# Regrouping the expert units of a mixture-of-experts stage: one 64-slot and two 32-slot experts per unit, large units and memory steps redistributed, half of the scatter moved

## The chip, the cores and the metric

The kernel runs on one core of a Trainium2 chip. The metric is the device time of the whole program in microseconds (us). Before the change it is 1763.9 us (median of three runs, 1759.8 to 1764.26).

The engines are named as in the profile: PE does matrix products (PEld is its weight load), DVE and ACT are the vector and the scalar engine, POOL is the general one, SP issues the loads of weights.

## What is computed

The program is one hybrid layer (sparse attention, a recurrent branch and a mixture of experts on 256 tokens of width 1024), then a second block of two layers with cross attention to a memory of 256 rows. The change touches the mixture of experts only. Cut to that:

```python
scores = sigmoid(hf @ router_w); choice = scores + router_bias
# 4 of 8 groups of experts, then the best 8 of 64 experts per token
top_e = top_k(where(emask, choice, -inf), 8)
gw = scores[top_e] / sum * 2.5
# every token, for each of its 8 experts e:
y[tok] += gw * (silu(h @ exp_gate[e]) * (h @ exp_up[e])) @ exp_down[e]
out = y + swiglu(h, sh_gate, sh_up, sh_down)
# later, for both layers of the second block:
k, v = split(rms_norm(mem) @ xa_wkv)
```

There are 64 experts; `exp_gate[e]` and `exp_up[e]` are 1024 x 256 and `exp_down[e]` is 256 x 1024, in float32: 1 MB each, 3 MB per expert. All 64 are always read, which is 192 loads of 1 MB.

## The kernel before, in words

**Units and pairs.** The expert stage is a list of *units* of 128 token slots. A unit holds one expert with 128 slots (letter H), two experts with 64 slots (S, the first four experts by number, and M) or four experts with 32 slots (L). All experts but the first four are ranked by how many tokens chose them, on the device: the 4 largest are H, the next 32 are M, the last 24 are L. An expert with more tokens than slots is finished in a loop behind the stage (`loop`), which runs no turn when there is no overflow. `GROUPS = "SMMMMLHLMHLMMM"` gives the order; each letter is a *pair* of units, so there are 14 pairs and 28 units, numbered from 0.

**What a unit does on PE.** At the start of a pair `gather` (L1821) makes the transposed tokens of 256 slots by 32 products with a one-hot matrix P, which DVE makes in `onehot` (L1807, L1808). Then per unit: `spread` (L1841) turns the slot weights; `up` (L1875) multiplies the tokens by the gate and then the up weights, 16 products per expert, each expert in its own columns of the array; ACT applies silu and DVE multiplies (f, L1881); `put` (L1914) adds the result of the unit *before* to the four accumulators of the output, 8 products of 512 columns; `turn` (L1889) transposes f and ACT copies it out (fT, L1891); `down` (L1904) multiplies by the down weights, 4 products per expert. So `put` of the unit before stands on PE between `up` and `turn`, in the time in which ACT and DVE make f; nothing stands between `turn` and `down`.

**Loads.** One queue (SP) issues all loads in program order. The loads of unit p+1 are put in front of the work of unit p. Each load takes the next of a ring of 14 buffers of 1 MB (3 base, 6 of `NRING2`, 3 of `NWS`, 2 of `NRING3`), so load n waits until the products that read load n-14 are done. An H unit takes 3 buffers, S and M take 6, L takes 12. For the last three units the base buffers leave the ring (`drop_ring`).

**Memory steps.** The keys and values of the second block's memory (`MemKV`) are worked out inside the stage, in nine steps behind the units of `KV_AT = 7, 9, 10, 11, 13, 14, 16, 17, 19`: a norm (1 load), two key steps and two value steps (2 loads each), then the same of the second layer but for its last value step, which runs behind the stage. Behind unit 8 stands `further()`, which plans the overflow on DVE and PE.

Of the kernel before, what the change touches and what calls it, by code (L numbers as in the profile page):

```python
# [10 lines left out]
F32 = mybir.dt.float32  # L11
# [4 lines left out]
OP = mybir.AluOpType  # L16
# [285 lines left out]
def flat(t):  # L302
    return t.rearrange("p k t -> p (k t)")
# [196 lines left out]
def mlp(K, layer, nm, nxt):  # L500
# [31 lines left out]


# [982 lines left out]
def first_h2(K, rs, rows, hh, hl):  # L1516


    nc, a = K.nc, K.a
    s2, b2 = rows  # L1520
    both = K.branch.tile([128, 2, D], F32, name="w", tag="w", bufs=2)
    for h in range(2):
        h2 = both[:, h]
        nc.vector.scalar_tensor_tensor(h2, K.X[:, h], rs[:, h:h + 1], s2, op0=OP.mult, op1=OP.mult)
        nc.vector.tensor_add(h2, h2, b2)
        v = h2.rearrange("p (q j) -> p j q", j=8)
        nc.scalar.activation(hh[:, h], v, AF.Copy)
# [26 lines left out]
NRING0, NRING2, NRING3, NRING4 = 6, 6, 2, 2  # L1554


NS, NH, NM, NL, NX = 4, 4, 32, 24, 32
C_PERM, C_FURTHER, NCOL = 64, 128, 128 + NX + 2
GROUPS = "SMMMMLHLMHLMMM"
KV_AT = 7, 9, 10, 11, 13, 14, 16, 17, 19  # L1560
FURTHER = 4


class Moe:
# [14 lines left out]
    def start(self):  # L1579

        K, nc, a = self.K, self.nc, self.a
        nc.gpsimd.dma_start(self.io, a["c_iota"])
        nm = K.nm2
        rs = nm.rows()
        PE, ACT = K.PE, K.ACT
        K.open("route", "right", cur=True)
        first_h2(K, rs, K.h2rows, self.hh, self.hl)
        next(K.parts[0], None)
        lT = K.t([64, T], "lgT")
        nc.scalar.activation(lT, K.lbank[:64, :T], AF.Copy)  # L1590
        lg = K.bank()
        for h in range(2):
            nc.tensor.transpose(lg[:, h * 64:h * 64 + 64], lT[:, h * 128:h * 128 + 128], K.ident[:64, :64])
        with K.after(PE):
            next(K.parts[1], None)
        up = [K.bank("acc") for _ in range(2)]
        rest = shared_in(K, "sh_up", up)
        next(rest)
        row = nm.row()
        s = K.t([128, 2, T], "shs")  # L1600
        self.hidden(K.gate, s, row, True)
        with K.after(PE):
            self.route(lg, rs)
        plan = self.plan()
        next(plan)
        self.take("S", tags=("tmp", "tmp", "acc"))
        next(plan, None)
        next(rest, None)
        self.hidden(up, s, row, False)
        with K.spare():  # L1610
            self.s = [K.t([128, 2, T], "sh" + p, 1, FR) for p in "hl"]
            K.split_into(*(flat(t) for t in self.s), flat(s))
        self.w = K.wload(a["sh_down"][0], 0, 2, 0, D)
        self.first = self.weights([0, 1])
# [182 lines left out]
                else:  # L1797
                    nc.vector.tensor_copy(o, b[:, h * NX:h * NX + NX])

    def onehot(self, col, n, w):  # L1800

        K, nc = self.K, self.nc
        sh = [128, 2, n, w]
        P, Pw = (K.t([128, 2, 256], x, 2, dt, pool=K.moep) for x, dt in (("P", FR), ("Pw", F32)))
        p, pw = (x[:, :, :n * w].rearrange("p h (n w) -> p h n w", w=w) for x in (P, Pw))
        pos, gw = (x[:, :, col:col + n][:, :, :, None].to_broadcast(sh) for x in (self.POS, self.GW))
        nc.vector.tensor_tensor(p, self.io[:, None, None, :w].to_broadcast(sh), pos, op=OP.is_equal)  # L1807
        nc.vector.tensor_tensor(pw, p.bitcast(F32), gw, op=OP.mult)  # L1808
        return P, Pw

    def gather(self, P, w, tags=("tmp",)):
# [16 lines left out]
                nc.scalar.activation(o, bv, AF.Copy)  # L1828
        return X

    def take(self, g, c=0, n=4, tags=("tmp",)):

        P, Pw = self.onehot(c + (C_PERM if g != "S" else 0), n, 256 // n)
        self.taken = self.gather(P, 256, tags), Pw

    def spread(self, Pw, unit):
# [25 lines left out]
                    d[n] = t.rearrange("p (j n) -> p j n", j=8)  # L1862
        return res

    def up(self, X, Pw, i, W):


        K, nc = self.K, self.nc
        C, g = self.spread(Pw, i)
        b = K.bank()  # L1870
        w = 128 // len(W)
        for x, n in enumerate(("exp_gate", "exp_up")):
            for k in range(8):
                for e, d in enumerate(W):
                    nc.tensor.matmul(b[w * e:w * e + w, x * 256:x * 256 + 256],  # L1875
                                     X[:, k, i * 128 + w * e:i * 128 + w * e + w], d[n][:, k],
                                     start=(x == 0 and k == 0), stop=(k == 7), skip_group_check=True)
        s = K.t([128, 256], "fs")
        nc.scalar.activation(s, b[:, 0:256], AF.Silu)  # L1879
        f = K.t([128, 256], "ff", 2)  # L1880
        nc.vector.scalar_tensor_tensor(f, b[:, 256:512], g, s, op0=OP.mult, op1=OP.mult)  # L1881
        return f, C
# [8 lines left out]
        nc.scalar.activation(flat(fT), b[:, :256], AF.Copy)  # L1891
        return fT

    def down(self, fT, W):

        K, nc = self.K, self.nc
        oh, ol = (K.t([128, 2, 512], "o" + p, 2, FR) for p in "hl")
        w = 128 // len(W)
        for n in range(2):
            b = K.bank()  # L1900
            for k in range(2):
                for e, d in enumerate(W):
                    s = slice(w * e, w * e + w)
                    nc.tensor.matmul(b[s], fT[:, k, s], d["exp_down"][:, k, n * 512:n * 512 + 512], start=(k == 0),  # L1904
                                     stop=(k == 1), skip_group_check=True)
            K.split_into(oh[:, n], ol[:, n], b)
        return oh, ol

    def put(self, C, parts, last=False):

        for h in range(2):
            for n in range(2):
                for x, o in enumerate(parts):
                    self.nc.tensor.matmul(self.y[2 * n + h], C[:, h * 128:h * 128 + 128], o[:, n], start=False,  # L1914
                                          stop=(last and x == 1), skip_group_check=True)

    def run(self, steps):

        K = self.K
        first = {"S": 0, "H": NS, "M": NS + NH, "L": NS + NH + NM}  # L1920
        units = []
        for g in GROUPS:
            n = {"H": 2, "L": 8}.get(g, 4)
            for i in range(2):
                units.append((g, first[g], n, [first[g] + i * n // 2 + e for e in range(n // 2)]))
            first[g] += n
        assert first == {"S": NS, "H": NS + NH, "M": NS + NH + NM, "L": 64}
        W, done = [self.first], None

        def load(p):  # L1930
            g, _, _, at = units[p]
            W.append(self.weights([r if g == "S" else self.idp[0:1, r:r + 1] for r in at]))

        for p, (g, c, n, _) in enumerate(units):
            if p % 2 == 0:
                if p:
                    self.take(g, c, n)
                X, Pw = self.taken
            more = steps[KV_AT.index(p)] if p in KV_AT else None
            if more:  # L1940
                more[0].load(more[1])
            if p + 1 < len(units):
                load(p + 1)
            w = W.pop(0)
            f, C = self.up(X, Pw, p % 2, w)
            with K.after(K.PE):
                if done:
                    self.put(*done)
                done = C, self.down(self.turn(f), w)
                if more:  # L1950
                    with K.after(K.PE):
                        more[0].step(more[1])
            if p == 2 * FURTHER:
                self.further()
            if p + 1 == len(units) - 3:
                self.end = self.ahead()
                K.drop_ring(K.ring)
        self.put(*done)
# [16 lines left out]
    def loop(self, end):  # L1975

        K, nc = self.K, self.nc
        with K.tc.For_i(0, end, 1):
            P, Pw = self.onehot(C_FURTHER, 2, 64)
            X = self.gather(P, 128)  # L1980
            W = self.weights([self.idx[0:1, e:e + 1] for e in range(2)])
            f, C = self.up(X, Pw, 0, W)
            self.put(C, self.down(self.turn(f), W))
# [139 lines left out]
```

## Time and profile before

| | |
|---|---|
| median of 3 runs | 1763.9 us |
| the profiled execution | 1768.93 us, span 1767.2 us |
| PE busy | 1678.5 us, 95% of the span |
| DVE, ACT, POOL busy | 834.3, 653.0, 85.7 us |
| moved by DMA | 418.99 MB, mean 237 GB/s |
| expert stage, first `up` to the end of the last `down` | 426.7 to 1004.8 us of the span |
| mean granted PE clock | 0.98 |

Busy time on PE is a sum of overlapping records, so 95% does not say that nothing could be saved there. The timeline gives, for one engine, start and duration of each instruction or run of like instructions, with the idle time before it and what ended that in brackets. A float32 product is recorded as two instructions: a `down` of M (8 products) is x16. The windows give busy time, granted clock and the share of the DMA engines for stretches of the span; a share of 1.00 or a little over means that the 16 DMA engines were never without a packet.

### The profile page before, as it was taken

How to read it: one execution, taken by the hardware profiler on the slowest of the kernel's cores; microseconds unless marked ns; L12 is line 12 of the kernel's file. 1: busy time of each engine (PE TensorE's matmuls, PEld its weight loads, DVE VectorE, ACT ScalarE, POOL GpSimd, SP SyncE). 2: the span in 40 equal slices, each digit the busy share in tenths (PEclk: the TensorE clock that was granted, in tenths of full speed). 3: DMA queues.
4: the chain of work that ended last, by engine and by line, in shares of the span. 5: the costliest groups of instructions: out<-in, count | busy, mean ns of one | idle time of the engine just before them, and what ended most of it. 6: DMA issues, size and time to landing. Idle time of an engine off the chain costs nothing. (4 is left out here: it accounts for less than half of the span.)

```text
span 1767.2 us, 27737 instructions
## 1 busy us (share of the span) xinstructions
PE 1678.5 (95%) x11326; PEld 1275.9 (72%) x11326; DVE 834.3 (47%) x1514; ACT 653.0 (37%) x1105; POOL 85.7 (5%) x105
## 2 busy tenths in 40 slices
PE   5999999998999999899989999999999999999997
PEld 2967667785566666467545577788999877989996
DVE  2664596675222211111112355666555667665554
ACT  2432444552112101211111255756444445554443
POOL 2000000103000000000000020202000000000000
PEclk9989799998999999999999999999999999999999
DMA  9454552583999799899699863546555533445551
GB/s 357 157 167 154 182 164 95 213 300 134 416 416 411 293 369 412 332 409 415 223 416 416 333 204 118 169 138 207 183 189 191 169 119 116 148 143 189 180 181 59
DMA packets 138317, 418.99 MB, mean 237 GB/s; under 512 B 10666, under 2 KB 17588, under 8 KB 118732
## 3 DMA queue, kind: packets, MB, share of 16 engines
q1 hardware_dynamic: 126272, 396.39, 61.0%
q0 software_dynamic: 4336, 12.34, 2.1%
q10 hardware_dynamic: 7580, 8.47, 1.7%
q8 instruction: 90, 1.47, 0.3%
q14 instruction: 39, 0.32, 0.1%
HBM read 410.88 MB, written 6.32 MB: 236 GB/s over the span
## 5 line engine op out<-in xcount | busy, mean ns | idle before, releaser
L153 DVE TENSOR_TENSOR w<-w 128x1024 fp32r<-128x1024 f32 (+1 forms) x283 | 347.2, 1229 | 263.3 <-ACT w L152 262.4
L152 ACT ACTIVATE w<-w 128x1024 fp32r<-128x1024 f32 (+1 forms) x285 | 300.0, 1054 | 317.0 <-PE acc L188 225.0
L1875 PE MATMUL tmp<-w 128*64 128x256 f32 (+2 forms) x2048 | 212.3, 391 | 8.7 <-DMA w<-in_exp_up_dram 7.9
L1875 PEld LDWEIGHTS tmp<-w 128*64 128x64 f32 (+2 forms) x2048 | 132.9, 133 | 79.2 <-issue 10.7
L188 PE MATMUL acc<-hTh,w 128*128 128x256 f32 (+2 forms) x552 | 160.5, 291 | 1.2 <-DVE w L153 1.2
L187 PE MATMUL acc<-hTl,w 128*128 128x256 f32 (+2 forms) x552 | 160.8, 292 | 0.2 <-DVE hTl L153 0.2
L186 PE MATMUL acc<-hTh,w 128*128 128x256 f32 (+2 forms) x552 | 159.9, 290 | 0.8 <-ACT hTh L152 0.7
L186 PE MATMUL tmp<-hTh,w 128*128 128x256 f32 x512 | 145.0, 283 | 0.0
L187 PE MATMUL tmp<-hTl,w 128*128 128x256 f32 x512 | 145.0, 283 | 0.0
L188 PE MATMUL tmp<-hTh,w 128*128 128x256 f32 x512 | 144.8, 283 | 0.0
L1904 PE MATMUL tmp<-w,fT 128*64 128x512 f32 (+2 forms) x512 | 111.3, 598 | 13.3 <-ACT fT L1891 13.3
L187 PEld LDWEIGHTS acc<-hTl,w 128*128 128x128 f32 (+1 forms) x552 | 106.8, 194 | 6.7 <-issue 5.8
L186 PEld LDWEIGHTS acc<-hTh,w 128*128 128x128 f32 (+1 forms) x552 | 106.8, 194 | 5.8 <-issue 4.2
L188 PEld LDWEIGHTS acc<-hTh,w 128*128 128x128 f32 (+1 forms) x552 | 106.7, 194 | 4.8 <-issue 2.6
L1881 DVE SCALAR_TENSOR_TENSOR ff<-tmp,gsl,fs 128x256 f32<-128x256 f32 x28 | 13.5, 483 | 188.6 <-ACT fs L1879 188.6
L187 PE MATMUL acc<-w,gh 128*128 128x512 f32 x256 | 102.2, 399 | 0.0
L186 PE MATMUL acc<-w,gh 128*128 128x512 f32 x256 | 100.9, 394 | 0.0
L188 PE MATMUL acc<-w,gl 128*128 128x512 f32 x256 | 100.5, 392 | 0.0
L153 DVE TENSOR_TENSOR ol<-tmp,oh 128x512 fp32r<-128x512 f32 x56 | 38.6, 690 | 128.2 <-ACT oh L152 128.1
L186 PEld LDWEIGHTS tmp<-hTh,w 128*128 128x128 f32 x512 | 97.9, 191 | 0.6
L187 PEld LDWEIGHTS tmp<-hTl,w 128*128 128x128 f32 x512 | 97.9, 191 | 0.5
L188 PEld LDWEIGHTS tmp<-hTh,w 128*128 128x128 f32 x512 | 98.0, 191 | 0.0
(633 smaller groups left out, 2917.6 us busy)
## 6 DMA issues: line engine op xcount, KB each, us to landing
w<-in_exp_gate_dram SPq DMA_DIRECT2D x64, 1024.0 KB, 13.3
w<-in_exp_up_dram SPq DMA_DIRECT2D x64, 1024.0 KB, 15.3
w<-in_exp_down_dram SPq DMA_DIRECT2D x64, 1024.0 KB, 13.4
w<-in_mlp_w_dram SPq DMA_DIRECT2D x64, 1024.0 KB, 5.3
w<-in_w_in_dram SPq DMA_DIRECT2D x23, 1024.0 KB, 6.0
adaw<-in_ada_w_dram SPq DMA_DIRECT2D x16, 1024.0 KB, 4.9
w<-in_xa_wkv_dram SPq DMA_DIRECT2D x16, 1024.0 KB, 11.0
w<-in_sb_w_in_dram SPq DMA_DIRECT2D x12, 1024.0 KB, 5.1
```

Source lines behind the costliest of these rows:

```text
L152: self.nc.scalar.activation(hi, src, AF.Copy)
L153: self.sub.tensor_tensor(lo, src, hi.bitcast(F32), op=OP.subtract)
L186: mm(out, lh, rh, start=first, stop=False, skip_group_check=True)
L187: mm(out, lh, rl, start=False, stop=False, skip_group_check=True)
L188: mm(out, ll, rh, start=False, stop=last, skip_group_check=True)
L1875: nc.tensor.matmul(b[w * e:w * e + w, x * 256:x * 256 + 256], X[:, k, i * 128 + w * e:i * 128 + w * e + w], d[n][:, k], start=(x == 0 and ...
L1881: nc.vector.scalar_tensor_tensor(f, b[:, 256:512], g, s, op0=OP.mult, op1=OP.mult)
L1904: nc.tensor.matmul(b[s], fT[:, k, s], d["exp_down"][:, k, n * 512:n * 512 + 512], start=(k == 0), stop=(k == 1), skip_group_check=True)
```

## The change

The experts are cut otherwise: 24 M and 32 L instead of 32 M and 24 L. A new unit X holds one M and two L experts (64 + 32 + 32 slots), so it takes 9 buffers. The order is `"SXXHXXMXXHXXM"`: 13 pairs, 26 units; no unit of four L experts is left. In an X unit every product has 32 columns: the 64-slot expert is cut in two products with the same weights. `onehot` makes P and Pw of an X pair in three pieces each. Half of `put` moves behind `turn`. The memory steps stand at other units.

```diff
-NS, NH, NM, NL, NX = 4, 4, 32, 24, 32
+NS, NH, NM, NL, NX = 4, 4, 24, 32, 32
-GROUPS = "SMMMMLHLMHLMMM"
-KV_AT = 7, 9, 10, 11, 13, 14, 16, 17, 19
+UNITS = {"S": "SS", "H": "H", "M": "MM", "X": "MLL"}
+WIDTH = {"S": 64, "H": 128, "M": 64, "L": 32}
+GROUPS = "SXXHXXMXXHXXM"
+KV_AT = 3, 5, 9, 11, 15, 16, 17, 21, 23
+def narrow(ws, W):
+    w = min(ws)
+    return [(w, d) for x, d in zip(ws, W) for _ in range(x // w)]
...
     def take(self, g, first, tags=("tmp",)):
+        off = 0 if g == "S" else C_PERM
+        if g == "X":
+            parts = [(0, 128, off + first["M"], 2, 1, 64), (64, 128, off + first["L"], 2, 2, 32)]
...
     def up(self, X, Pw, i, W, ws):
...
-                for e, d in enumerate(W):
-                    nc.tensor.matmul(b[w * e:w * e + w, x * 256:x * 256 + 256],
-                                     X[:, k, i * 128 + w * e:i * 128 + w * e + w], d[n][:, k],
+                at = 0
+                for w, d in narrow(ws, W):
+                    nc.tensor.matmul(b[at:at + w, x * 256:x * 256 + 256], X[:, k, i * 128 + at:i * 128 + at + w],
+                                     d[n][:, k], start=(x == 0 and k == 0), stop=(k == 7), skip_group_check=True)
+                    at += w
...
-    def put(self, C, parts, last=False):
-        for h in range(2):
+    def put(self, C, parts, halves=(0, 1), last=False):
+        for h in halves:
...
             with K.after(K.PE):
                 if done:
-                    self.put(*done)
-                done = C, self.down(self.turn(f), w)
+                    self.put(*done, halves=(0,))
+                fT = self.turn(f)
+                if done:
+                    self.put(*done, halves=(1,))
+                done = C, self.down(fT, w, ws)
```

PE's order of unit 2, from its `up` to its `down`, in the program before (`oh`, `ol` are the two parts of the output of unit 1, `C` its scatter matrix):

```order
L1875 MATMUL tmp<-w 64x256 x32
L1914 MATMUL acc<-oh,C 128x512
L1914 MATMUL acc<-ol,C 128x512
L1914 MATMUL acc<-oh,C 128x512
L1914 MATMUL acc<-ol,C 128x512
L1914 MATMUL acc<-oh,C 128x512
L1914 MATMUL acc<-ol,C 128x512
L1914 MATMUL acc<-oh,C 128x512
L1914 MATMUL acc<-ol,C 128x512
L1889 MATMUL tmp<-ident,ff 128x128 x2
L1904 MATMUL tmp<-w,fT 64x512 x8
```

The same place in the changed program, where unit 2 is the first X unit (L1898 is `up`, L1937 `put`, L1912 `turn`, L1926 `down`):

```order
L1898 MATMUL tmp<-w 32x256 x64
L1937 MATMUL acc<-oh,C 128x512
L1937 MATMUL acc<-ol,C 128x512
L1937 MATMUL acc<-oh,C 128x512
L1937 MATMUL acc<-ol,C 128x512
L1937 MATMUL acc<-oh,C 128x512
L1912 MATMUL tmp<-ident,ff 128x128 x2
L1937 MATMUL acc<-ol,C 128x512
L1937 MATMUL acc<-oh,C 128x512
L1937 MATMUL acc<-ol,C 128x512
L1926 MATMUL tmp<-w,fT 32x512 x16
```

Three of the eight `put` products stand behind `turn` now, and `up` and `down` have twice as many products of half the columns.

SP's order where the loads of one M unit stand, in the program before (the first row is the last load of the unit ahead of it; ISA rows are SP's own register work):

```order
L1858 DMA w_4417<-in_exp_down_dram 128x2x1024
L1861 ISA
L1861 DMA w_4555<-in_exp_gate_dram 128x2048
L1861 ISA
L1861 DMA w_4557<-in_exp_gate_dram 128x2048
L1861 ISA
L1861 DMA w_4559<-in_exp_up_dram 128x2048
L1861 ISA
L1861 DMA w_4561<-in_exp_up_dram 128x2048
L1858 ISA
L1858 DMA w_4563<-in_exp_down_dram 128x2x1024
```

And in the changed program, from the last load of unit 3 on: the load of the memory itself, which stood ahead of unit 8's loads before, and then the loads of unit 4, an X unit:

```order
L1881 DMA w_4348<-in_exp_down_dram 128x2x1024
L355 DMA w_4463<-in_mem_2_dram 128x2x1024
L1884 ISA
L1884 DMA w_4492<-in_exp_gate_dram 128x2048
L1884 ISA
L1884 DMA w_4494<-in_exp_gate_dram 128x2048
L1884 ISA
L1884 DMA w_4496<-in_exp_gate_dram 128x2048
L1884 ISA
L1884 DMA w_4498<-in_exp_up_dram 128x2048
```

A unit brings three loads of each kind where M brings two, in the same order of kinds, and the memory step comes four units earlier.

## Rows read from the trace of the kernel before

**Rows 1.** Windows: length, busy per engine (count), PEclk, DMA share, GB/s.
```profile
498.00:530.00 32.00, 31.05 (x223) 19.07 (x223) 8.03 (x15) 5.12 (x10) 0.00 (x0) 1.00 1.02 417
584.00:617.00 33.00, 32.53 (x186) 23.84 (x186) 5.42 (x12) 2.97 (x7) 1.15 (x2) 0.94 0.69 258
739.00:765.00 26.00, 21.45 (x195) 11.91 (x194) 3.13 (x6) 3.50 (x9) 0.00 (x0) 0.93 1.02 416
748.20:754.00 5.80, 5.73 (x60) 3.06 (x61) 0.00 (x0) 0.36 (x1) 0.00 (x0) 0.71 1.03 411
```
**Rows 2.** Timeline of PE, one M unit: start, duration, engine, line, tiles.
```profile
543.18 0.44 PE L1841 MATMUL tmp<-ident,Pw 128*128 128x128 f32 x2
543.55 7.13 PE L1875 MATMUL tmp<-w 128*64 128x256 f32 x64
550.61 0.50 PE L1914 MATMUL acc<-oh,C 128*128 128x512 f32 x1
...
551.87 0.39 PE L1914 MATMUL acc<-ol,C 128*128 128x512 f32 x1
...
552.56 0.38 PE L1889 MATMUL tmp<-ident,ff 128*128 128x128 f32 x2
553.41 3.65 PE L1904 MATMUL tmp<-w,fT 128*64 128x512 f32 x16 [0.47 <-ACT fT L1891]
557.00 2.17 PE L375 MATMUL tmp<-ident,w 128*128 128x128 f32 x16
```
**Rows 3.** Timeline of PE, a gather: its first product and what follows its last.
```profile
525.53 0.39 PE L1821 MATMUL tmp<-P,h2h 128*128 128x256 f32 x1
...
529.41 0.38 PE L1841 MATMUL tmp<-ident,Pw 128*128 128x128 f32 x2
```
**Rows 4.** The page's group of all down products.
```profile
L1904 PE MATMUL tmp<-w,fT 128*64 128x512 f32 (+2 forms) x512 | 111.3, 598 | 13.3 <-ACT fT L1891 13.3
```
**Rows 5.** Timeline of PE: turn of unit 0 (no put ahead), up of unit 2.
```profile
444.32 0.44 PE L1889 MATMUL tmp<-ident,ff 128*128 128x128 f32 x2 [1.03 <-DVE ff L1881]
...
466.79 7.13 PE L1875 MATMUL tmp<-w 128*64 128x256 f32 x64
```
**Rows 6.** Timeline of PE: a key step, an L unit's up, a value step.
```profile
599.61 14.08 PE L393 MATMUL tmp<-kvT,w 128*128 128x256 f32 x64
...
618.03 7.11 PE L1875 MATMUL tmp<-w 128*32 128x256 f32 x128
...
661.20 14.00 PE L412 MATMUL tmp<-w,kvT 128*128 128x512 f32 x32
```
**Rows 7.** Timeline of PE: spread of units 15 and 21, and the next up.
```profile
738.88 0.38 PE L1841 MATMUL tmp<-ident,Pw 128*128 128x128 f32 x2
...
748.27 5.33 PE L1875 MATMUL tmp<-w 128*32 128x256 f32 x58 [1.91 <-DMA w<-in_exp_up_dram]
...
768.06 7.13 PE L1875 MATMUL tmp<-w 128*64 128x256 f32 x64
...
886.02 0.44 PE L1841 MATMUL tmp<-ident,Pw 128*128 128x128 f32 x2
...
914.61 1.73 PE L1875 MATMUL tmp<-w 128*64 128x256 f32 x14
```
**Rows 8.** Timeline of SP's queue: first load into a reused buffer; last expert loads.
```profile
440.02 1.01 SPq L1861 DMA_DIRECT2D w<-in_exp_up_dram  x2
...
974.00 7.57 SPq L1858 DMA_DIRECT2D w<-in_exp_down_dram  x2
```
**Rows 9.** The page's DMA issues: count, size of each, us from issue to landing.
```profile
w<-in_exp_gate_dram SPq DMA_DIRECT2D x64, 1024.0 KB, 13.3
```
**Rows 10.** Groups of DVE by line: the second one-hot instruction of each pair.
```profile
L1808 DVE TENSOR_TENSOR Pw<-P,gw 128x512 f32<-128x512 f32 x14 | 9.5, 680 | 0.0
```
**Rows 11.** Timeline of PE: the overflow plan behind unit 8, and unit 9's spread.
```profile
577.09 0.19 PE L1760 MATMUL tmp<-nbb,trib 64*64 64x1 bf16 x1
...
583.77 0.69 PE L1841 MATMUL tmp<-ident,Pw 128*128 128x128 f32 x2
```

More of the change, by code (lines that the diff above doesn't have):

```diff
@@ L1605, in start @@
         next(plan)
-        self.take("S", tags=("tmp", "tmp", "acc"))
+        self.take("S", {"S": 0}, tags=("tmp", "tmp", "acc"))
         next(plan, None)
@@ L1798, in further, with onehot @@
                     nc.vector.tensor_copy(o, b[:, h * NX:h * NX + NX])
-    def onehot(self, col, n, w):
+    def onehot(self, parts):
         K, nc = self.K, self.nc
-        sh = [128, 2, n, w]
         P, Pw = (K.t([128, 2, 256], x, 2, dt, pool=K.moep) for x, dt in (("P", FR), ("Pw", F32)))
[L1805 to L1808, printed above, removed]
+        for at, step, col, n, m, w in parts:
+            for i in range(n if m > 1 else 1):
+                k = m if m > 1 else n
+                sh = [128, 2, k, w]
+                if m > 1 or step == w:
+                    c = slice(at + i * step, at + i * step + k * w)
+                    p, pw = (x[:, :, c].rearrange("p h (n w) -> p h n w", w=w) for x in (P, Pw))
+                else:
+                    p, pw = (x[:, :, at:].rearrange("p h (n w) -> p h n w", w=step)[:, :, :n, :w] for x in (P, Pw))
+                pos, gw = (x[:, :, col + i * m:col + i * m + k][:, :, :, None].to_broadcast(sh) for x in (self.POS, self.GW))
+                nc.vector.tensor_tensor(p, self.io[:, None, None, :w].to_broadcast(sh), pos, op=OP.is_equal)
+                nc.vector.tensor_tensor(pw, p.bitcast(F32), gw, op=OP.mult)
         return P, Pw
@@ L1829, in gather, with take @@
         return X
-    def take(self, g, c=0, n=4, tags=("tmp",)):
-        P, Pw = self.onehot(c + (C_PERM if g != "S" else 0), n, 256 // n)
+    def take(self, g, first, tags=("tmp",)):
+        off = 0 if g == "S" else C_PERM
+        if g == "X":
+            parts = [(0, 128, off + first["M"], 2, 1, 64), (64, 128, off + first["L"], 2, 2, 32)]
+        else:
+            w = WIDTH[g]
+            parts = [(0, w, off + first[g], 256 // w, 1, w)]
+        P, Pw = self.onehot(parts)
         self.taken = self.gather(P, 256, tags), Pw
@@ L1863, in weights, with up @@
         return res
-    def up(self, X, Pw, i, W):
+    def up(self, X, Pw, i, W, ws):
         K, nc = self.K, self.nc
@@ L1870, in up @@
         b = K.bank()
-        w = 128 // len(W)
         for x, n in enumerate(("exp_gate", "exp_up")):
             for k in range(8):
-                for e, d in enumerate(W):
-                    nc.tensor.matmul(b[w * e:w * e + w, x * 256:x * 256 + 256],
-                                     X[:, k, i * 128 + w * e:i * 128 + w * e + w], d[n][:, k],
-                                     start=(x == 0 and k == 0), stop=(k == 7), skip_group_check=True)
+                at = 0
[3 more added lines that the diff above has]
+                    at += w
         s = K.t([128, 256], "fs")
@@ L1892, in turn, with down @@
         return fT
-    def down(self, fT, W):
+    def down(self, fT, W, ws):
         K, nc = self.K, self.nc
         oh, ol = (K.t([128, 2, 512], "o" + p, 2, FR) for p in "hl")
-        w = 128 // len(W)
         for n in range(2):
@@ L1901, in down @@
             for k in range(2):
[L1902 to L1905, printed above, removed]
+                at = 0
+                for w, d in narrow(ws, W):
+                    nc.tensor.matmul(b[at:at + w], fT[:, k, at:at + w], d["exp_down"][:, k, n * 512:n * 512 + 512],
+                                     start=(k == 0), stop=(k == 1), skip_group_check=True)
+                    at += w
             K.split_into(oh[:, n], ol[:, n], b)
         return oh, ol
-    def put(self, C, parts, last=False):
-        for h in range(2):
+    def put(self, C, parts, halves=(0, 1), last=False):
+        for h in halves:
             for n in range(2):
@@ L1922, in run @@
         for g in GROUPS:
-            n = {"H": 2, "L": 8}.get(g, 4)
+            begin = dict(first)
             for i in range(2):
-                units.append((g, first[g], n, [first[g] + i * n // 2 + e for e in range(n // 2)]))
-            first[g] += n
+                at = []
+                for c in UNITS[g]:
+                    at.append(first[c])
+                    first[c] += 1
+                units.append((g, begin, at, [WIDTH[c] for c in UNITS[g]]))
         assert first == {"S": NS, "H": NS + NH, "M": NS + NH + NM, "L": 64}
@@ L1930, in load @@
         def load(p):
-            g, _, _, at = units[p]
+            g, _, at, _ = units[p]
             W.append(self.weights([r if g == "S" else self.idp[0:1, r:r + 1] for r in at]))
-        for p, (g, c, n, _) in enumerate(units):
+        for p, (g, begin, _, ws) in enumerate(units):
             if p % 2 == 0:
                 if p:
-                    self.take(g, c, n)
+                    self.take(g, begin)
                 X, Pw = self.taken
@@ L1944, in run @@
             w = W.pop(0)
-            f, C = self.up(X, Pw, p % 2, w)
+            f, C = self.up(X, Pw, p % 2, w, ws)
             with K.after(K.PE):
                 if done:
-                    self.put(*done)
-                done = C, self.down(self.turn(f), w)
+                    self.put(*done, halves=(0,))
[3 more added lines that the diff above has]
+                done = C, self.down(fT, w, ws)
                 if more:
@@ L1978, in loop @@
         with K.tc.For_i(0, end, 1):
-            P, Pw = self.onehot(C_FURTHER, 2, 64)
+            P, Pw = self.onehot([(0, 64, C_FURTHER, 2, 1, 64)])
             X = self.gather(P, 128)
             W = self.weights([self.idx[0:1, e:e + 1] for e in range(2)])
-            f, C = self.up(X, Pw, 0, W)
-            self.put(C, self.down(self.turn(f), W))
+            f, C = self.up(X, Pw, 0, W, (64, 64))
+            self.put(C, self.down(self.turn(f), W, (64, 64)))
             for i, t in enumerate((self.POS[:, :, C_FURTHER:], self.GW[:, :, C_FURTHER:], self.idx[:, None, :NX + 2])):
```

## Prediction

> **What bounds the kernel now.** I read the page's busy shares first, then the windows over the expert stage, then PE's timeline, then SP's queue. In the stage two resources take turns. In [rows 1] the stretch 498 to 530 has the DMA engines at 1.02 with 417 GB/s while PE is busy 31.05 of 32 us: both full. From 584 to 617 the DMA share is 0.69 at the same busy PE: the ring is full and PE sets the pace, because a key step of 14.08 us asks for only two loads [rows 6]. From 739 to 765 the share is 1.02 again and PE is busy only 21.45 of 26 us: an L pair waits for its loads. So the stage loses twice, the DMA idles where memory steps stand close together, and PE waits in the second unit of each late L pair.
>
> What a load costs: 1024 KB [rows 9], 1.049 MB, at 417 GB/s is 2.52 us. What a unit costs on PE: 543.18 to 557.00, 13.8 us [rows 2]. Of that 0.47 us is the wait of `down` for fT; the page's sum of 13.3 us over 28 units is the same 0.47 each [rows 4]. A gather is 525.53 to 529.41, 3.9 us [rows 3].
>
> **Term 1, two units and one gather fewer.** 28 units become 26 and 14 gathers 13: 2 x 13.8 + 3.9 = **31.5 us** of PE. The work per unit does not change: `up` takes 7.13 us with 64 columns [rows 2] and 7.11 us with 32 [rows 6], so an X unit with twice the products of an M unit takes the same. Cutting the 64-slot expert in two streams its weights from the buffer twice, without another DMA.
>
> The Trainium skill, "TensorE: Matmul & The Clock Gate", Measured speedup vs the span model, has four tiles side by side at 3.07 times one, not 4. By that X units would be 4/3.07 slower, an estimate of 16 x 0.30 x (7.1 + 3.7) = 52 us, and the change would lose. The trace of L units (7.11 us) disagrees, and I follow it.
>
> **Term 2, half of `put` behind `turn`.** The order shows five products ahead of `turn` and three behind. Behind: `down` starts 0.85 us after `turn`, of which `turn` fills 0.38 us and the wait 0.47 us [rows 2]; three products at the spacing (551.87 - 550.61) / 5 = 0.25 us fill 0.75 us. The wait goes. Ahead: `turn` needs f, and with no `put` at all it waited 1.03 us for DVE [rows 5]; five products fill 1.26 us. Nothing replaces the wait. 25 units have a `put` there (not the first): 25 x 0.47 = **11.7 us**. If f came later, the term would be between 0 and 11.7; I take the whole, since DVE and ACT are mostly idle beside `put`. A unit is then 13.35 us.
>
> **Term 3, waits for loads.** Before: unit 15 and the gather behind it take from 738.88 to 768.06 = 29.2 us, unit 21 from 886.02 to 914.61 = 28.6 us [rows 7]. Undisturbed: 13.8 + 3.9 + 0.4 = 18.1 us. So 11.1 + 10.5 = 21.6 us are lost there now. Part is clock: behind the wait the granted clock of a 5.8 us window is 0.71 [rows 1], time at the lower of its two levels, 1.2 GHz, which costs 0.29 x 5.8 = 1.7 us per place.
>
> After: the balance of a pair is PE's time less its loads. X pair: 2 x 13.35 + 3.9 - 18 x 2.52 = -14.8. H pair: 30.6 - 15.1 = +15.5. M pair: 30.6 - 30.2 = +0.4. Key or value step: 14.1 - 5.0 = +9.1. Norm: 2.2 - 2.5 = -0.3. The overflow plan, 577.09 to 583.77 [rows 11]: +6.7.
> - First place, pairs 1 and 2 (X X behind S). The 15th load goes out at 440.02 [rows 8] in both programs, and the ring is drained from there without a pause, so load n lands at about 442 + (n - 14) x 2.52. Unit 5's last is n = 6+6+9+9+1+9+9 = 49: 530.2. PE: unit 2 starts `up` at 466.79 [rows 5] less 0.5; unit 3 at 479.7; with norm and gather unit 4 at 499.1 and unit 5 at 512.4; its `down` 9.4 us later at 521.8. **8.4 us late**, met in units 4 and 5, each with its slow clock: 8.4 + 2 x 1.7 = 11.8.
> - Then from 0: key +9.1, H +15.5, X -14.8, plan +6.7, key +9.1, X -14.8, value +9.1, M +0.4, X -14.8, value +9.1, X -14.8, norm -0.3: -0.5 at unit 17. It closes to about nothing in the mean, with loads in groups of three. I take half of what a place costs now, 5.4 + 1.7 = 7.1.
> - Behind: key, H, X, key, X, value: +9.1 + 15.5 - 14.8 + 9.1 - 14.8 = +4.1 at the lowest, no wait. The greatest lead, 25.6 us, is 10 loads, which the ring can hold.
>
> After 18.9, before 21.6: **2.7 us** won. Ends: all gone (21.6 won), or every X pair but the three that follow an H, M or S pair with a lead late (5 x 10.8 = 54, so 32.4 lost).
>
> **At nothing.** The one-hot of an X pair is six DVE instructions for two of 680 ns [rows 10]: at most 4 x 0.68 = 2.7 us more per pair, in a pair of 30 us in which DVE is busy for 8 of 32 us [rows 1]; uncovered 8 x 2.7 = 22 us. SP issues nine loads per unit instead of six, 192 in all as before. Memory steps cost the same and only stand elsewhere. By the reference's routing on its own inputs the largest expert that now gets 32 slots has 28 tokens, so the overflow loop makes no turn, as now; one turn would be a unit and a gather, some 18 us.
>
> **Sum.** 31.5 + 11.7 + 2.7 = 45.9. The profiled execution of 1768.9 becomes 1723.0. It lies 5.0 above the median of the runs, so the time is 1763.9 - 45.9 = **1718**.
>
> **Rivals.**
> - A, only Term 1 and 3 hold: f is late, `turn` waits instead of `down`. Against it: 1.26 over 1.03 us. 1718 + 11.7 = 1730. Chance 0.10.
> - B, the waits are gone: the balance of -0.5 and the 8.4 us speak against it. 1718 - 18.9 = 1699. Chance 0.08.
> - C, X pairs wait in five places: units of nine loads leave only five buffers ahead, so a load is held until a product ends. For it: the DMA share of 0.69 where the ring was full. Against: 1.02 through the L pair, whose unit holds twelve. 1718 + 2.7 + 32.4 = 1753. Chance 0.10.
> - D, slower: the same ring holds the DMA back so much that it sets the end. From 440.0 to 981.6 [rows 8] 194 loads go out (192 + 2 + 14 less 14), 489 us of transfer: 90% of 541.6 us. In the new order about 8 us of PE follow the last load. It becomes slower by 0.3% when the last load goes out past 1002, that is below 87%. At 84% (489 / 0.84 = 582, end at 1030 against 1004.8): 1789. Chance 0.05.
> - E, the products of 32 columns cut from one expert do not run side by side as those of four experts do, so the change does not do what it says: then an X unit's products take half as long again, 16 x 5.4 = 86 us: 1804. The L unit of [rows 6] speaks against it. Chance 0.01.
>
> For D there is a rule as well: the Trainium skill, "DMA: Bandwidth & Descriptors", Where 436 GB/s comes from, has HBM loads bound at about 358 GB/s. By it a load is 2.93 us (an estimate), 194 loads end at 1010, and the time would be about 1776. The trace's 417 GB/s over 32 us disagrees.
>
> **Chances.** The forecast has 0.66, with its own range 1708 to 1728 (Term 3 from 10 better to 10 worse). A measurement of this kernel can tell 0.3%, 5 us, from no change. Faster: forecast, A, B and C, 0.94, less 0.01 for the far end of C, 0.93; same 0.02, that end and the near end of D; slower 0.05, the rest of D and E. The range 1698 to 1742 takes in A and B and leaves out C, D and E, 0.16.
>
> **What would show it.** 26 units of 13.3 to 13.5 us on PE where no load is late; `up` of X at 7.1 us; no bracket in front of `down`, and none in front of `turn`; waits for exp_up or exp_down in units 4, 5 and 17 and nowhere else; DMA share near 1.0 from 440 to about 930; the last `down` ends near 959. The prediction is wrong if DMA waits stand in most X pairs, if the DMA share falls under 0.9, or if `up` of X takes more than 7.3 us.

## The result, and the profile after

The changed kernel takes 1737.3 us (median of four runs, 1731.5 to 1738.0) where before took 1764.1 (four runs, 1759.8 to 1766.6): a ratio of 0.9843, 95% interval 0.9815 to 0.9872. Run again on another chip it took 1731.7 against 1767.5, 0.9796 (0.9776 to 0.9816). So 27 to 36 us were won, where 45.9 were forecast. The profiled execution took 1731.5 us, span 1728.5.

The work on PE is as forecast. The timeline of PE in the changed kernel, a whole X unit (start, duration, engine, line, tiles; answers to [rows 2, 6]):

```profile
475.07 7.11 PE L1898 MATMUL tmp<-w 128*32 128x256 f32 x128
482.12 0.50 PE L1937 MATMUL acc<-oh,C 128*128 128x512 f32 x1
...
483.39 0.38 PE L1912 MATMUL tmp<-ident,ff 128*128 128x128 f32 x2
483.52 0.47 PE L1937 MATMUL acc<-ol,C 128*128 128x512 f32 x1
...
484.39 3.66 PE L1926 MATMUL tmp<-w,fT 128*32 128x512 f32 x32
```

`up` takes 7.11 us, no bracket stands ahead of `turn` (L1912) or `down` (L1926), and the second half of `put` (L1937) lies between them. The page's groups of `down` (answers to [rows 4]) and `up`: busy time, mean ns of one, idle time before them and what ended it:

```profile
L1926 PE MATMUL tmp<-w,fT 128*32 128x512 f32 (+2 forms) x640 | 103.7, 597 | 0.5 <-ACT fT L1914 0.5
L1898 PE MATMUL tmp<-w 128*32 128x256 f32 (+2 forms) x2560 | 203.5, 390 | 13.7 <-DMA w<-in_exp_up_dram 8.5
```

The 13.3 us in front of `down` are 0.5 now. A unit takes 13.25 us where it took 13.8. The waits for weights stand where they were expected, in units 4, 5 and 17. Timeline of PE (answers to [rows 7]):

```profile
500.97 3.64 PE L1898 MATMUL tmp<-w 128*32 128x256 f32 x58 [1.90 <-DMA w<-in_exp_up_dram]
...
516.10 3.65 PE L1898 MATMUL tmp<-w 128*32 128x256 f32 x62 [1.86 <-DMA w<-in_exp_gate_dram]
...
523.58 5.33 PE L1898 MATMUL tmp<-w 128*32 128x256 f32 x58 [1.89 <-DMA w<-in_exp_up_dram]
...
776.29 3.65 PE L1898 MATMUL tmp<-w 128*32 128x256 f32 x62 [1.87 <-DMA w<-in_exp_gate_dram]
```

The brackets are short, but a late unit is long because its products trickle in as the weights land. From one `turn` to the next, less 13.25 and what else stands between, the places cost 13.8 us in units 4 and 5, 9.1 in unit 17 and 0.8 in unit 23: 23.7 us, where 18.9 were forecast and 21.6 stood before.

What decides is one window from the first load of unit 2's weights to the last load of the memory's weights. First before, then the changed kernel (stretch, length, busy per engine, granted clock, DMA share, GB/s):

```profile
438.85:986.53 547.68, 522.34 (x3588) 331.35 (x3589) 107.94 (x221) 83.82 (x175) 9.07 (x16) 0.99 0.95 377
```

```profile
434.41:940.80 506.39, 487.82 (x4163) 303.33 (x4163) 101.94 (x232) 78.33 (x164) 9.08 (x16) 0.99 1.01 409
```

This *stream* is 198 loads, 180 of expert weights and 18 of the memory steps, about 207 MB in both. Before, the DMA moved it at 377 GB/s with a share of 0.95; it had gaps to give. Now the share is 1.01. In windows of 20 us from 435 to 935 it is 1.01 to 1.03 but for four, of which one is the start and these are the others (the changed kernel):

```profile
575.00:595.00 20.00, 20.00 (x213) 11.91 (x212) 5.14 (x9) 3.75 (x7) 0.00 (x0) 1.00 0.97 390
635.00:655.00 20.00, 20.00 (x272) 10.54 (x271) 5.44 (x14) 2.29 (x5) 0.00 (x0) 1.00 0.98 385
835.00:855.00 20.00, 20.00 (x211) 12.13 (x213) 4.74 (x9) 3.94 (x8) 0.00 (x0) 1.00 0.94 376
```

In these three PE is busy throughout, and SP's queue waits up to 7.1, 7.5 and 7.1 us for `up` products: the ring is full there. Before, windows of 20 us went down to 0.54.

Where the time went, from the two profiled executions. I call *stage* the time from unit 0's `turn` to the end of the last `down`:

| stretch | before | after | difference |
|---|---|---|---|
| start of the span to unit 0's `turn` | 444.3 | 439.9 | -4.4 |
| the stage | 560.5 | 520.4 | -40.1 |
| last `down` to the second block's first transpose (L326) | 18.3 | 23.3 | +5.0 |
| the rest of the span | 744.1 | 744.9 | +0.8 |

The first row is no gain. In 13 traces the start of the shared expert's products lies anywhere from 416.2 to 424.6 us, before 423.5 and after 417.5; the runs that start late do so in either order of the program, and the differences arise in steps between 40 and 245 us, among instructions that the change does not touch. Without it the difference is 34.3 us, between the 27 and 36 of the two pairs of medians.

The third row is a cost nobody had forecast: the value step behind the overflow loop starts later and runs at a lower granted clock.

```profile
967.75 15.89 PE L412 MATMUL tmp<-w,kvT 128*128 128x512 f32 x32 [5.30 <-DMA w<-in_ev_w_in_dram]
```

Before it stood at 1009.18, took 14.00 us and waited 2.21. The granted clock during it was 1.00 before and 0.88 after.

### The profile page after: what moved, and what is told of

Its sections match the earlier page's. It is cut to its first block, busy times and chain, and to the rows that moved or that the text cites. A ratio compares the mean times of both kernels' runs of the same rounds, so it can differ in the third digit from the quotient of the medians.

```text
span 1728.5 us, 28908 instructions
## 1 busy us (share of the span) xinstructions
PE 1649.3 (95%) x11910; PEld 1250.7 (72%) x11910; DVE 831.7 (48%) x1532; ACT 648.1 (37%) x1095; POOL 85.7 (5%) x105
## 5 line engine op out<-in xcount | busy, mean ns | idle before, releaser
L1898 PE MATMUL tmp<-w 128*32 128x256 f32 (+2 forms) x2560 | 203.5, 390 | 13.7 <-DMA w<-in_exp_up_dram 8.5
L1898 PEld LDWEIGHTS tmp<-w 128*32 128x32 f32 (+2 forms) x2560 | 120.0, 120 | 86.7 <-issue 13.1
L186 PE MATMUL acc<-hTh,w 128*128 128x256 f32 (+2 forms) x552 | 160.7, 292 | 1.7 <-ACT w L152 1.0
L186 PE MATMUL tmp<-hTh,w 128*128 128x256 f32 x512 | 145.0, 283 | 0.0
L186 PEld LDWEIGHTS acc<-hTh,w 128*128 128x128 f32 (+1 forms) x552 | 108.1, 196 | 7.1 <-issue 4.5
L1926 PE MATMUL tmp<-w,fT 128*32 128x512 f32 (+2 forms) x640 | 103.7, 597 | 0.5 <-ACT fT L1914 0.5
L186 PE MATMUL acc<-w,gh 128*128 128x512 f32 x256 | 100.9, 394 | 0.0
L186 PEld LDWEIGHTS tmp<-hTh,w 128*128 128x128 f32 x512 | 97.7, 191 | 0.6
L1902 ACT ACTIVATE fs<-tmp 128x256 f32<-128x256 f32 x26 | 10.0, 384 | 223.7 <-PE tmp L1898 223.7
```

The source lines that it names most:

```text
L186: mm(out, lh, rh, start=first, stop=False, skip_group_check=True)
L1898: nc.tensor.matmul(b[at:at + w, x * 256:x * 256 + 256], X[:, k, i * 128 + at:i * 128 + at + w], d[n][:, k], start=(x == 0 and k == 0), sto ...
L1926: nc.tensor.matmul(b[at:at + w], fT[:, k, at:at + w], d["exp_down"][:, k, n * 512:n * 512 + 512], start=(k == 0), stop=(k == 1), skip_grou ...
```

## The experiments

Two theories stood after the result. **P**: PE still sets the end of the stage; the rest of the forecast was lost in the late places, behind the loop, and where a `down` is cut. In four pairs of X units the next unit's `spread` stands inside `down`, behind 6 of its 16 products. **L**: the loads set the end, and what is taken off PE comes back as waits. All ratios are to the kernel before on the same chip.

**1. The changed kernel again** (`repeat`, no edit).

> The changed kernel once more, unchanged, to see how much of the difference between its traced execution (38.7 us shorter in span than that of before) and its median (26.8 us shorter) is scatter between executions, and whether the 4.4 us earlier start of the expert stage and the 5.3 us wait of the last value step behind the stage come again. Both theories: 1737 within 5 us. Theory L (loads set the end of the expert stage now: the DMA share is 1.00 to 1.02 from 435 to 945 us): the share is at 1.0 again. Theory P (PE still sets it, and the rest of the gain is lost on PE, 1.7 us in each X pair whose down is cut in two by the next spread, and in the late places): the same two late places, at units 4 and 5 and at unit 17.

1731.7 us (1727.6 to 1735.7), ratio 0.9796 (0.9776 to 0.9816), stage 521.3, waits at the same places. The pattern is the program's; the total differs from chip to chip by about 0.5%.

**2. The scatter in one piece** (`put_whole`).

```diff
-                    self.put(*done, halves=(0,))
+                    self.put(*done)
                 fT = self.turn(f)
-                if done:
-                    self.put(*done, halves=(1,))
```

> The changed kernel with all eight scatter products ahead of turn again. Units grow by 0.58 us of PE, 25 x 0.58 = 14.5 us. Theory P: 12 to 15 us slower than the changed kernel (about 1751). Theory L: most of it goes into the waits for loads, 0 to 6 us slower (1737 to 1743).

1742.7 us, ratio 0.9862 (0.9842 to 0.9883), 11 us over `repeat`. But in the two profiled executions 6.1 of these lie ahead of the stage, in the scatter of the start. The stage is 526.2 against 520.4 and 521.3: 5 to 6 us. An undisturbed unit takes 13.79 us again, so 25 x 0.54 = 13.5 us went back onto PE, and less than half of that reached the end of the stage.

**3. The split scatter alone, in the kernel before** (`before_half`).

```diff
-                    self.put(*done)
+                    self.put(*done, halves=(0,))
                 fT = self.turn(f)
+                if done:
+                    self.put(*done, halves=(1,))
```

> The kernel before with only the second half of the scatter moved behind turn. 27 x 0.58 = 15.7 us of PE. Theory P: 13 to 16 us faster than before (1748 to 1751), since PE sets the pace nearly everywhere in the kernel before. Theory L says the same of stretches where the ring is full, but nothing where loads are late: 8 to 13 us faster (1751 to 1756).

1756.9 us, ratio 0.9935 (0.9916 to 0.9954). Stage 551.0, 9.5 us less than before. Here 27 units each became about 0.5 us shorter (13.81 to 13.30 from `turn` to `turn`), 13.8 us in all. So Term 2 is real; about two thirds of it reached the end where the DMA has gaps, and less than half behind the regrouping.

**4. The changed kernel with the memory steps where they were** (`old_kv`).

```diff
-KV_AT = 3, 5, 9, 11, 15, 16, 17, 21, 23
+KV_AT = 7, 9, 10, 11, 13, 14, 16, 17, 19
```

> The changed kernel with the memory steps at the units of the kernel before (7, 9, 10, 11, 13, 14, 16, 17, 19). Theory L: the steps stand close together, the ring fills, the DMA idles there and the lost transfer time comes back at the end: 8 to 20 us slower, with a DMA share under 0.9 in the middle of the stage. Theory P: late places move, 0 to 5 us slower.

1735.0 us, ratio 0.9822 (0.9807 to 0.9838), 3.3 over `repeat`. Some waits moved (new ones at 761.6 and from 912 to 920 us), the stage is 521.1. The gap in the loads that was written for L came: from 855 to 875 us the share is 0.68, and the stream takes 511.8 us, 5.4 more than in the changed kernel. The cost written for L, 8 to 20 us, did not: from the last load to the end of the last `down` it is 14.8 us instead of 19.5. A later last load that has less work behind it costs next to nothing.

**5. No cut `down`** (`spread_second`).

```diff
-        C, g = self.spread(Pw, i)
+        with K.after(*[K.PE] * i):
+            C, g = self.spread(Pw, i)
```

> Edit: the spread of a pair's second unit is placed behind the last product, so that the down of units 2, 10 and 14 is no longer cut after 6 of its 16 products (the pair 22/23 stays cut by the read of a table's row). Theory P (TensorE sets the end, each cut costs 1.7 us): these pairs take 26.5 us instead of 28.2, the stage about 5 us less than in the changed kernel, some 1727 us on a chip where the changed kernel takes 1732. Theory L (the loads set the end): the time won comes back as a wait for a load in the next late unit, 0 to 2 us less in all.

1734.3 us, ratio 0.9811 (0.9786 to 0.9836): nothing is won. The cut does cost time. Timeline of PE in the changed kernel, units 10 and 11, where `up` of unit 11 follows `down` of unit 10 at 650.77:

```profile
645.10 1.92 PE L1926 MATMUL tmp<-w,fT 128*32 128x512 f32 x12
646.95 0.44 PE L1864 MATMUL tmp<-ident,Pw 128*128 128x128 f32 x2
647.31 2.33 PE L1926 MATMUL tmp<-w,fT 128*32 128x512 f32 x17
...
650.77 7.07 PE L1898 MATMUL tmp<-w 128*32 128x256 f32 x116
```

and in `spread_second`, the same `down` in one piece and, further on, unit 15:

```profile
651.03 3.66 PE L1927 MATMUL tmp<-w,fT 128*32 128x512 f32 x32
655.00 7.11 PE L1899 MATMUL tmp<-w 128*32 128x256 f32 x128
...
734.02 3.64 PE L1899 MATMUL tmp<-w 128*32 128x256 f32 x58 [0.41 <-DMA w<-in_exp_up_dram]
739.86 5.47 PE L1927 MATMUL tmp<-w,fT 128*32 128x512 f32 x32
```

From `turn` to `turn` the pair takes 13.3 us where the cut one took 14.95: 1.7 us won. Unit 15, which had not waited, now does, and its `down` takes 5.47 us instead of 3.66. The stage is 522.0. What was won on PE is paid back at the next late load.

**6. Fewer loads** (`fewer_loads`): 16 of 64 loads of down weights left out, the third expert of an X unit uses the second's.

```diff
                 if n == "exp_down" and len(ids) == 3 and d is res[2]:
                     d[n] = res[1][n]
                     continue
```

> In units of three experts the third uses the second's exp_down weights, so 16 fewer transfers of 1 MB, about 40 us of the stage's 510 us of transfers; the output then lacks the third expert's own exp_down. Theory P: the 23.7 us of waits for loads in units 4, 5 and 17 go, and nothing else, so 20 to 24 us less than the changed kernel. Theory L: the stage gets shorter by nearly all of the transfer time taken away, 30 to 40 us.

1709.1 us, ratio 0.9673 (0.9637 to 0.9708). Stage 497.4, 23.0 less, with one late place left (6 us, unit 5), and no `down` is cut in the order that the edit gives. That is P's number (20 to 24). The 30 to 40 us of L did not come; with nearly all waits gone it is PE that sets the end now. This gives PE's own length of the stage, about 497 - 6 = 491 us, or 496 with the three cut `down`s of the changed kernel (1.7 us each). Loads and PE lie close together, and this run alone would not tell the theories apart.

**7. Less work on PE: half of the scatter** (`half_scatter`): the second half of `put` is left out, so half of the sums are missing.

```diff
-                if done:
-                    self.put(*done, halves=(1,))
```

> The second half of the scatter's products behind each unit is left out (half of each expert's rows are not added to the result): about 25 x 0.9 = 22 us less work on TensorE in the stage. Theory P: 18 to 22 us less than the changed kernel less what comes back as later loads in units 4, 5 and 17 (up to 7 us), so 13 to 22. Theory L: the transfers need the same time, 0 to 6 us less.

1726.3 us, ratio 0.9763 (0.9734 to 0.9792); stage 520.5, the same as with the whole scatter. The experiment was weaker than planned: without products behind `turn` the bracket of 0.47 us is back, and a unit is only 0.2 us shorter. The total is about 6 us lower than `repeat`'s by the ratios, but 3.3 of these stand behind the last `down`, where the value step waits 2.2 us instead of 5.3.

**8. Much less work on PE: half of `up`** (`half_up`): 4 of 8 steps, so the sums lack half of the inputs.

```diff
-            for k in range(8):
+            for k in range(4):
```

> The up of every unit takes 4 of its 8 steps (the sums over the other half of the inputs are left out, so the output lacks them); every load stays. TensorE loses about 26 x 3.5 = 91 us of the stage's work. Theory P (TensorE sets the stage's end but for the late places): the stage loses 60 to 90 us. Theory L (the loads set it): the stage stays within 10 us of the changed kernel's 520, with the time taken away from TensorE back as waits for weights, and the DMA share at 1.0 up to the last load.

1719.2 us, ratio 0.9729 (0.9700 to 0.9758). About 91 us of products are gone, and by the ratios the time falls by 12 to 20 us. The stage is 513.6, 7 less; from the shared expert's first product (L186) to the last `down`'s end it is 530.9 against 542.8, 12 less. Timeline of PE in unit 3, which never waited before, and the window over its stream:

```profile
466.20 1.91 PE L1898 MATMUL tmp<-w 128*32 128x256 f32 x26 [1.03 <-DMA w<-in_exp_gate_dram]
468.88 0.63 PE L1898 MATMUL tmp<-w 128*32 128x256 f32 x4 [0.76 <-DMA w<-in_exp_up_dram]
471.36 0.62 PE L1898 MATMUL tmp<-w 128*32 128x256 f32 x2 [1.86 <-DMA w<-in_exp_up_dram]
473.87 3.62 PE L1898 MATMUL tmp<-w 128*32 128x256 f32 x26 [1.90 <-DMA w<-in_exp_up_dram]
```

```profile
432.54:935.03 502.49, 451.35 (x2927) 258.66 (x2929) 102.50 (x233) 79.10 (x166) 9.11 (x16) 0.95 1.02 413
```

The stream takes 502.5 us, 4 less than with the whole `up`, and no window of 20 us up to 935 is under a share of 1.01. What follows the last load takes 13.1 us instead of 19.5. This decides for L: in the changed kernel the loads set the end, and PE's work still costs time only behind the last load and in the short places where the ring is full.

**9. 64 + 32 + 32 columns instead of four times 32** (`mixed`).

```diff
-    w = min(ws)
-    return [(w, d) for x, d in zip(ws, W) for _ in range(x // w)]
+    return list(zip(ws, W))
```

> Units of one 64-slot and two 32-slot experts with products of 64, 32 and 32 columns instead of four sets of 32: the same units, order and loads. If products of 32 columns run as fast side by side as those of 64 and the kernel's gain is from the grouping alone, up and down take the same time as before the change's narrowing and the total is within 5 us of the changed kernel. If the narrow form itself carries gain, three sets side by side leave 32 of 128 columns' worth of rows to a longer turn: up of 7.1 us becomes up to 9 to 10.6 us in each of the 16 X units, 30 to 56 us slower than the changed kernel; with loads as the limit (theory L) less of it shows, 10 to 25 us.

1962.6 us, ratio 1.1103 (1.1073 to 1.1133): far outside what was expected. Timeline of PE, an X unit's `up` and `down`:

```profile
464.49 18.18 PE L1897 MATMUL tmp<-w 128*64 128x256 f32 x96
...
484.87 8.01 PE L1925 MATMUL tmp<-w,fT 128*64 128x512 f32 x24
```

A quarter fewer products (48 for 64 in `up`, each recorded as two) take 18.18 us instead of 7.11, and those of `down` 8.0 to 8.6 instead of 3.66. 16 units x (11.1 + 4.4) = 248 us more, less the 24 us of waits that vanish, is 224; by the ratios it is 223 to 231. The equal widths are no detail of the change, the regrouping rests on them.

**10. `spread` of every unit behind the last product** (`spread_after`).

```diff
-        C, g = self.spread(Pw, i)
+        with K.after(K.PE):
+            C, g = self.spread(Pw, i)
```

> The spread of every unit stands behind the last product, that of unit 0 too: unit 0's up then runs in one piece behind the shared expert's 24 products, not between them. Unit 0's up and those products took about 22 us from 417.5 to 439.9 in the changed kernel, with a product of the other shape every microsecond; apart they should take 5.2 + 7.1 = 12.3 and the wait for the transposes, some 13 to 15 us. The pieces of up's weights come free 6 to 9 us earlier, so the loads start earlier by so much. Theory L: the whole stage moves ahead with them, 6 to 9 us less in all. Theory P: the same 7 to 9 us from the shorter start and about 5 more from the three pairs whose down is no longer cut, 12 to 14 us less than the changed kernel.

1726.4 us, ratio 0.9763 (0.9741 to 0.9785). In the changed kernel unit 0's `up` and the shared expert's products alternate. Timeline of PE, the last such turn and the rest of that `up`,

```profile
433.31 0.65 PE L1898 MATMUL tmp<-w 128*64 128x256 f32 x2
433.88 0.49 PE L188 MATMUL acc<-w,shl 128*128 128x512 f32 x1
434.31 4.54 PE L1898 MATMUL tmp<-w 128*64 128x256 f32 x40
439.88 0.44 PE L1912 MATMUL tmp<-ident,ff 128*128 128x128 f32 x2 [1.03 <-DVE ff L1904]
```

and the same `up` in `spread_after`:

```profile
422.26 7.13 PE L1899 MATMUL tmp<-w 128*64 128x256 f32 x64
430.42 0.44 PE L1913 MATMUL tmp<-ident,ff 128*128 128x128 f32 x2 [1.03 <-DVE ff L1905]
```

From the shared expert's first product to unit 0's `turn` it is 14.2 us instead of 22.4, and unit 2's first weights are asked for 5.9 us behind that product instead of 16.9. The stage itself is 520.8, as in the changed kernel: it has only moved ahead, with the loads. From the same first product to the last `down`'s end it is 535.0 instead of 542.8, so 7.7 us are won, L's 6 to 9 and not P's 12 to 14. The totals alone, 6 us by `repeat` and 14 by the first measurement, would not tell.

**11. Another order of the pairs besides** (`best`).

```diff
-GROUPS = "SXXHXXMXXHXXM"
-KV_AT = 3, 5, 9, 11, 15, 16, 17, 21, 23
+GROUPS = "SXHXXXMXMHXXX"
+KV_AT = 3, 7, 8, 10, 12, 15, 20, 21, 22
```

> spread_after, and another order of the pairs (S X H X X X M X M H X X X instead of S X X H X X M X X H X X M) with the memory steps at units 3, 7, 8, 10, 12, 15, 20, 21 and 22. The early X pairs are parted by an H pair, which needs a third of an X pair's bytes and nearly its products, and X pairs stand at the end, where TensorE has fallen behind the loads by some 15 us in the changed kernel. Theory L: what TensorE does behind the last load shrinks from 15 us to 6 to 10, so 5 to 9 us less than spread_after. Theory P: the waits of 23.7 us go from their places and less than 10 come back elsewhere: 10 to 17 us less than spread_after.

1717.1 us (1715.1 to 1719.3), ratio 0.9710 (0.9688 to 0.9733): faster than both kernels, by 0.5% more than `spread_after` and about 1% more than the change. The window over its stream, and PE in the last unit:

```profile
429.76:936.80 507.04, 496.24 (x4207) 309.29 (x4205) 104.92 (x241) 80.09 (x168) 9.08 (x16) 0.99 1.02 412
```

```profile
934.97 0.62 PE L1899 MATMUL tmp<-w 128*32 128x256 f32 x2 [1.34 <-DMA w<-in_exp_up_dram]
937.92 5.33 PE L1899 MATMUL tmp<-w 128*32 128x256 f32 x58 [2.34 <-DMA w<-in_exp_up_dram]
...
945.44 3.80 PE L1927 MATMUL tmp<-w,fT 128*32 128x512 f32 x32
```

The units 4 and 5 no longer wait and the stream runs at 412 GB/s; the last unit waits for its own weights, as it must when loads set the end. From the shared expert's first product to the end it is 526.9 us, 8.1 less than `spread_after`, which is L's 5 to 9. Cut into the time to the first load of unit 2, the stream and what follows its last load, that is 7.5 + 507.0 + 12.4 against 5.9 + 508.9 + 20.2: the order of the pairs paid almost wholly behind the last load.

**12. The shared expert's products behind unit 0's `up`** (`up_first`, on top of `best`).

```diff
-        with K.later(0), K.spare():
-            self.shared()
...
             f, C = self.up(X, Pw, p % 2, w, ws)
+            if p == 0:
+                with K.after(K.PE), K.spare():
+                    self.shared()
```

> The kernel of the run best, with the shared expert's 24 products moved behind unit 0's up (before its turn). The 5.4 us of products no longer stand ahead of unit 0's up, so its weights come free up to 5 us earlier, and the first weights of unit 2 are asked for so much earlier. Theory L: the stream of loads starts and ends 3 to 5 us earlier, and the kernel takes 3 to 5 us less than best, about 1712 to 1714 where before takes 1769. Theory P: TensorE does the same work and only the 1.5 us of waits around unit 0's turn are covered, 0 to 2 us less.

1723.4 us, ratio 0.9771 (0.9747 to 0.9796): slower than `best`, against both theories' numbers. The two ran on different chips, so the traces have to show why, and they show L's reason. SP's queue in `up_first`,

```profile
431.90 0.39 SPq L1879 DMA_DIRECT2D w<-in_exp_down_dram  x1
433.35 1.48 SPq L1882 DMA_DIRECT2D w<-in_exp_gate_dram  x3
```

and in `best`:

```profile
426.95 0.92 SPq L1881 DMA_DIRECT2D w<-in_exp_down_dram  x2
429.76 4.15 SPq L1884 DMA_DIRECT2D w<-in_exp_gate_dram  x3
```

The plan's product (L1745 in `up_first`, L1747 in `best`) comes ahead of all this in both, at 415.93 and 421.27. Behind it the first weights of unit 2 are asked for after 17.4 us in `up_first` and 8.5 in `best`. PE was early, but the shared expert's products stopped twice for weights split late by ACT and POOL (1.20 us at 428.74, 1.25 at 431.18) and ended at 433.3, and the first load of unit 2 goes out right behind them, as it does in `best` at 429.76. It goes out 8.9 us later, and the last `down` ends 8.1 us later behind the same mark (536.1 against 528.0).

## Why the prediction was right, and where it was not

**Direction, range, the work per unit: right.** 26 units of 13.25 us, `up` of X at 7.1 us, no bracket ahead of `turn` or `down`, waits in units 4, 5 and 17, the DMA near 1.0 from 435 to 935. Term 1 and Term 3 together were to save 34.2 us; `put_whole` has just these two, with the longer units that need the loads less soon, and its stage is 34.3 us shorter than before's. That the two agree so closely is in part chance, since `put_whole` has the three cut `down`s as well. Rivals D and E did not come: in windows of 20 us the DMA share was never under 0.94 up to 935, and 32 columns do run four side by side: `up` takes 7.11 us in four tiles and 7.07 in the one of an H unit, so the 4/3.07 that the prediction weighed against Term 1 does not show. Neither did A, whose sign was a wait ahead of `turn`, nor C with its five late places.

The size was not as good. 1737.3 lies in the range 1698 to 1742, but outside the forecast's own 1708 to 1728; it was caught by the room that the range left for A, which is not what happened. That much of the hit is luck.

**Term 2** was priced at 0.47 us for each of 25 units; the unit lost 0.54, 13.5 us in all. In the old grouping, with 27 such units, 9.5 us of 13.8 reached the end. In the new one 5 to 6 of 13.5 did. The size was right on PE and wrong at the end of the stage.

**The step that failed is Term 3's balance**, and with it "18.9, before 21.6". It treated a late place as a local loss that is made good behind it ("It closes to about nothing in the mean"). What it left out is the sum over all loads. The forecast's stage of 560.5 - 45.9 = 514.6 us, with the first load 5.5 us ahead of it and 19.5 us of work behind the last, leaves 500.6 us for 198 loads, 2.53 us each; the 5.5 and 19.5 are the changed kernel's own. The 2.52 us came from a full stretch of 32 us ([rows 1], 417 GB/s). Over a whole stream the changed kernel got 409 GB/s, 2.56 us each, 506.4 us. The 5.8 us between are the stage's 520.4 against 514.6. So the forecast asked the loads for their best rate throughout, without saying so: a division of bytes by time, made for rival D with the old length, was not made for the new one. `half_up`, whose stream had no pause, took 502.5 us for the same loads. By that 1.9 of the 5.8 us are the rate, and 3.9 are the places where the ring was full, an estimate. The prediction had said that the ring can hold its greatest lead, 25.6 us; the three pauses lie at the three highest leads of its own balance, behind the two H pairs (24.6 each) and behind the key step of unit 9 (25.6).

**The rest** is the 5.0 us behind the loop, whose cause is open, and 0.8 elsewhere. 45.9 - 5.8 - 5.0 - 0.8 = 34.3.

Unforeseen, but without effect, were the cut `down`s: three at 1.7 us on PE, hidden as soon as the loads decide.

## What to carry to other kernels

Before summing savings on one engine, divide the bytes that the stage must move by the time that is left; where the quotient comes near the best rate seen, every further saving on the engine is worth little, however real it is. Then the levers are when the first load goes out (7.7 us won where it went out 11 us earlier), what stands behind the last load (7.8 us less in `best`), and fewer bytes. To see which resource decides, take away far too much of one: half of `up` said in one run what savings of 5 us could not.

## What the runs showed of the hardware that was not expected

- Products on column tiles of unequal width (64, 32, 32) took 18.18 us for 48, four of 32 columns 7.11 us for 64 (each recorded as two). Why was not tried apart.
- A `down` of 32-column products that is cut by two full-width transposes behind 6 of its 16 products makes its pair 1.7 us longer (14.95 against 13.3 us); the same transposes between whole sequences do not.
- Alternating products of two shapes is dear: a turn of one shared product and one of `up`, recorded as two, took 1.0 us, where apart the records are spaced at 0.23 and 0.11 us, 0.45 in all. If the change of shape is the cost here and the change of width in `mixed`, it is (1.0 - 0.45) / 2 = 0.28 us a change here and 11.1 / 32 = 0.35 us there, with two changes in each of 16 steps. That both have one cause is not shown.
- The loads of one core held 409 to 413 GB/s over 500 us, and 417 in the 32 us of [rows 1]. The rule of 358 GB/s that the prediction set beside rival D does not hold here. The Trainium skill, "Perfetto Trace Analysis", Roofline, has the ceiling of a single active core at about 435 GB/s, that of its 16 DMA engines; the traces agree that it is above 358 and stay below 435. By that figure 207 MB would take 476 us, an estimate; no run here moved them in less than 502 us.
- The start of the value step behind the overflow loop, which waits on no semaphore in the program: idle 2.2 us in before, `before_half`, `half_scatter` and `half_up`, 5.2 to 5.7 in the others. In `half_up`:

```profile
952.49 15.70 PE L412 MATMUL tmp<-w,kvT 128*128 128x512 f32 x32 [2.19 <-DVE u L2025]
```

Its longer run (15.70 against 14.00 us before, at a granted clock of 0.89) stays with the short wait, so the two have different causes. The label that names a load does not explain either. This was not settled.
